# Four spacer tiles that shift tile addresses modulo 256 bytes in a one-core hybrid decoder layer

## The chip, the cores and the metric

The kernel runs on one core of a Trainium2 chip. The metric is the time of one execution on the device in microseconds (us), as the median of several runs. A profile of one execution shows which engine did what and when: PE is TensorE (matmul), PEld its loading of weights, DVE is VectorE, ACT ScalarE, POOL GpSimd, SP the engine that issues most transfers. Numbers such as L158 are lines of the kernel.

## The reference

The kernel computes one layer on a sequence of 1024 tokens of width 1024, in float32:

```python
hn = rmsnorm(x, attn_norm_w)
proj = hn @ w_in                                   # 1024 x 3592
da_q, da_k, da_v, ml_qk, ml_v, ml_o, ml_i, ml_f = split_projection(proj)
da_out = diff_attention(da_q, da_k, da_v, lam, slopes)   # 4 heads, causal, ALiBi
da_out = rmsnorm(da_out, diff_norm_w) * (1.0 - lam_init)
qk = silu(causal_dwconv(ml_qk, mlstm_conv_w, mlstm_conv_b))
h = mlstm_chunkwise(mq, mk * ML_DIM ** -0.5, mv, i_pre, logf)   # 4 heads
ml_out = sigmoid(ml_o) * rmsnorm(h, mlstm_norm_w)
x = x + concatenate([da_out, ml_out]) @ w_out
u = causal_dwconv(rmsnorm(x, ffn_norm_w) @ w_up, ffn_conv_w, ffn_conv_b)   # D_FF = 2816
gate, up = split(u, 2)
x = x + (silu(gate) * up) @ w_down
return rmsnorm(x, final_norm_w)
```

## The kernel before

**Products.** A float32 operand is split into a high and a low part in a rounded type (fp32r), and each product is three matmuls: high by high, high by low, low by high. `mm3` (L157) keeps the two halves of a weight tile in the array and streams the token tile; `mm3b` (L162) keeps the token tile in the array and streams the weight tile. A matmul has 128 rows, 128 columns of weights and, nearly always, 512 streamed columns. While one streams, PEld reads the weights of the next from the on-chip memory (SBUF).

**Stages.** In order of time:

- Projections: x transposed and normalised is split into 16 tiles `xb` (L208, pool `px`). Columns of w_in come through `wf`, are split into `w` (8 buffers, pool `wp`, L121), and are multiplied by `xb`. The gates are 32 matmuls with `wg16` as weights, 16 columns for each block kc of 128 inputs (L411). While these run, POOL forms sums of weight blocks that later stages use (L327).
- mLSTM in eight chunks, then attention in 32 steps of a head and 128 tokens. The query and key projections of a head, which still read `xb`, are put between the steps. In the last head `px` is closed, and `px2` and `pmx` open at its place.
- Output projection: `mixT` (L799) loads a row block of the mixed heads into `mx`, transposes it on PE against an identity in `cst` and splits it into `mxT`; `mxT` is then held in the array, and `w` or `th` (the weights of the attention half) stream.
- MLP, up: a seven-product scheme in place of eight block products. The tokens stand in blocks: B11 and B21 in `hb` (pool `ph0`), B22 in `B22h` and `B22l`, and the sums T1 to T4 with their high parts in `th` and their low parts in `raw` (all pool `phn`) or in `x2a` (pool `px2`). Sums of weights are made on POOL by `up_sums` (L968 to L970), in tiles `s` and `wu` of pool `pf`, which takes the place of `pmx`. `product` (L1013) issues the matmuls.
- MLP, down: a second scheme of the same kind from `wf`, `bw`, `a12`, `a21`, `a22`, split into `w`, and the final norm.

**Order.** The order of the work is written by hand in the program: each engine executes its instructions in program order, and waits on semaphores for those of others. SP issues the loads and stores in one queue.

**Addresses.** The pools are stacks. Those of the left side grow upwards from the pool below; those opened with `side="right"` grow downwards. Within a pool the first tile takes the lowest address. Sizes are rounded up to 32 bytes. One spacer exists already: `padr`, 64 bytes at the top of the right side. As built, nearly every large tile begins at 160 modulo 256; the exceptions are `cst` (128), `vext` (96 and 128 for its two buffers) and `Cst` (64). The slices that a matmul reads are whole multiples of 512 bytes in, so they keep the tile's place; only `wg16` steps by 64 bytes from one kc to the next, and the slices of `vext` and `Cst` by 516 bytes.

`Scope` (L51) is a pool that can be closed by hand:

Of the kernel before, what the change touches and what calls it, by code (L numbers as in the profile page):

```python
# [17 lines left out]
P = 128  # L18
# [21 lines left out]
def tile_hybrid(ctx: ExitStack, tc: tile.TileContext, I: dict, out: bass.AP):  # L40
# [105 lines left out]
    def getw(ahead):  # L146
        n = used[0]
        used[0] += 1
        while len(made) < min(n + 1 + ahead, len(specs)):
            made.append(wpiece(*specs[len(made)]))  # L150
        return made[n]
# [14 lines left out]


    px = Scope("px")
    pr0 = Scope("pr0", side="right")
    pq = Scope("pq", side="right")  # L170
    pa = Scope("pa", side="right")
# [507 lines left out]
    def qk_units(h):  # L679

        hd = Head()

        def alloc():
            for n in ("qs0", "qs1", "ks0", "ks1", "kl"):
                setattr(hd, n, pat.t([P, S], F32R, n, 2))

        def proj(which, hf):
            if hf == 0:
                if which == "q":
                    alloc()  # L690
                hd.w = getw(1)
            ps = mmps()
            for kc in range(KC):
                st_mm(ps, hd.w, kc, hf)
            t = slice(hf * 512, (hf + 1) * 512)
            f = pat.t([P, 512], tag="qf", bufs=2)
            V.scalar_tensor_tensor(f, ps, -0.125 / SLOPE[h] if which == "q" else 1.0, RB[:, t], op0=ALU.mult, op1=ALU.mult)
            a0, a1 = (hd.qs0, hd.qs1) if which == "q" else (hd.ks0, hd.ks1)
            lo = pat.t([P, 512], F32R, "qlo") if which == "q" else hd.kl[:, t]
            for a, p in ((a0, slice(0, 64)), (a1, slice(64, 128))):  # L700
                A.activation(a[p, t], f[p, :], AF.Copy)
                (V if h == 0 else GP).tensor_tensor(lo[p, :], f[p, :], a[p, t].bitcast(F32), op=ALU.subtract)
            s0, s1 = (lo[0:64, :], lo[64:128, :]) if which == "q" else (a0[0:64, t], a1[64:128, t])
            nc.sync.dma_start(a0[64:128, t].bitcast(F32), s0.bitcast(F32))
            nc.sync.dma_start(a1[0:64, t].bitcast(F32), s1.bitcast(F32))

        return hd, [lambda w_=w_, f=f: proj(w_, f) for w_ in "qk" for f in range(2)]
# [8 lines left out]
    def pad_q(n):  # L716
        if n < len(seq):
            h, qt = seq[n]
            for c, a in ((0, heads[h].qs0), (1, heads[h].qs1)):
                r = slice(c * 64, (c + 1) * 64)  # L720
                GP.tensor_copy(qz[c][n % 2][r, :], a[r, qt * P:(qt + 1) * P])
# [10 lines left out]
    def attn_scores(h, qt):  # L732
        hd = heads[h]
        L = (qt + 1) * P
        qs_ = slice(qt * P, (qt + 1) * P)
        if qt == 0:
            st[h] = {"Z": sm8(16, "Z"), "ss": sm8(8, "ass")}
        e = st[h]
        if qt % 4 == 0:
            e["O", qt // 4] = pat.t([P, 4, P], tag="O", bufs=2)  # L740
        mn, mb_ = sm8(2, "mn"), sm8(2, "mb")
        pt = []
        for c in range(2):
            sps = big([P, S])
            z = qz[c][qt % 2]
            qs, ks = (hd.qs0, hd.ks0) if c == 0 else (hd.qs1, hd.ks1)
            for c0 in range(0, L, 512):
                js = slice(c0, c0 + max(256, min(512, L - c0)))
                PE.matmul(sps[:, js], qs[:, qs_], ks[:, js], start=True, stop=False)
                PE.matmul(sps[:, js], z, hd.kl[:, js], start=False, stop=True)  # L750
            s = pat.t([P, S], tag="s", bufs=4)
            V.tensor_tensor_reduce(s[:, :L], sps[:, :L], B0[:, S - L:S], op0=ALU.add, op1=ALU.min, accum_out=mn[:, c:c + 1], scale=1.0, scalar=3.0e38)  # L752
            V.tensor_scalar(mb_[:, c:c + 1], mn[:, c:c + 1], SLOPE[h], None, op0=ALU.mult)  # L753
            A.activation(s[:, :L], s[:, :L], AF.Exp, bias=mb_[:, c:c + 1], scale=-SLOPE[h], accum_out=e["Z"][:, c * 8 + qt:c * 8 + qt + 1])  # L754
            pt.append(s)
        e["p", qt] = pt

    def attn_out(h, qt):
        e = st[h]
        L = (qt + 1) * P  # L760
        pt = e.pop(("p", qt))
        cc = sm8(1, "cc")
        V.reciprocal(cc, e["Z"][:, 8 + qt:9 + qt])
        V.scalar_tensor_tensor(cc, cc, nlam, e["Z"][:, qt:qt + 1], op0=ALU.mult, op1=ALU.mult)
        a = pt[0]
        V.scalar_tensor_tensor(a[:, :L], pt[1][:, :L], cc, a[:, :L], op0=ALU.mult, op1=ALU.add)
        ops = psA.t([P, P], tag="sb")
        for b0 in range(0, qt + 1, 4):
            nb = min(4, qt + 1 - b0)
            tps = psA.t([P, 512], tag="sa")  # L770
            for b in range(nb):
                PE.transpose(tps[:, b * P:(b + 1) * P], a[:, (b0 + b) * P:(b0 + b + 1) * P], ident)
            aT = pat.t([P, 512], tag="aT", bufs=2)
            A.activation(aT[:, :nb * P], tps[:, :nb * P], AF.Copy)  # L774
            for b in range(nb):
                k = b0 + b
                PE.matmul(ops, aT[:, b * P:(b + 1) * P], vda[k // 2][:, k % 2, h * P:(h + 1) * P], start=k == 0, stop=k == qt)  # L777
        o = e["O", qt // 4][:, qt % 4, :]
        A.activation(o, ops, AF.Square, accum_out=e["ss"][:, qt:qt + 1])
        A.activation(o, ops, AF.Copy)  # L780

    def attn_finish(h, q0, q1):
        n = q1 - q0
        e = st[h]
        r0, v = sm8(n, "r0"), sm8(n, "av")
        V.reciprocal(r0, e["Z"][:, q0:q1])
        V.tensor_tensor(v, r0, r0, op=ALU.mult)
        V.tensor_tensor(v, v, e["ss"][:, q0:q1], op=ALU.mult)
        y = rsqrt(meps(v, n, 128, "t"), n, "t")
        f = sm8(n, "af")  # L790
        V.tensor_tensor(f, y, r0, op=ALU.mult)
        o = e["O", q0 // 4][:, q0 % 4:q0 % 4 + n, :]
        GP.tensor_tensor(o, o, f.unsqueeze(2).broadcast_to([P, n, P]), op=ALU.mult)
        nc.sync.dma_start(mixed[q0:q1, :, h * P:(h + 1) * P].rearrange("t p d -> p t d"), o)
# [4 lines left out]
    def mixT(tt, half, bank):  # L799
        m = pmx.t([P, 512], tag="mx", bufs=2)  # L800
        nc.sync.dma_start(m, mixed[tt, :, half * 512:(half + 1) * 512])
        tps = bank()
        for i in range(4):
            PE.transpose(tps[:, i * P:(i + 1) * P], m[:, i * P:(i + 1) * P], ident)
        t = pmx.t([P, 2, 512], F32R, "mxT", 2)
        A.activation(t[:, 0, :], tps, AF.Copy)
        V.tensor_tensor(t[:, 1, :], tps, t[:, 0, :].bitcast(F32), op=ALU.subtract)
        return t
# [8 lines left out]
    def add_proj(tt, t, w):  # L817
        xx = x2[tt]
        for hf in range(2):
            ps = mmps()  # L820
            oproj(t, w, hf, ps)
            c = slice(hf * 512, (hf + 1) * 512)
            V.tensor_tensor(xx[:, c], xx[:, c], ps, op=ALU.add)

    def load_x2(tt):
        xx = px2.t([P, D], tag="x2a" if tt < 4 else "x2b", bufs=4)
        nc.sync.dma_start(xx, I["x"][tt])
        x2.append(xx)

    def oml_unit(tt):  # L830
        if tt == 0:
            w_oml.extend(getw(0) for i in range(4))
        load_x2(tt)
        add_proj(tt, mixT(tt, 1, mmps), w_oml)
# [4 lines left out]
    for n, (h, qt) in enumerate(seq):  # L839
        if qt == 0:  # L840
            if h < H - 1:
                heads[h + 1], fill = qk_units(h + 1)
            else:
                px.close()
                px2 = Scope("px2")
                pmx = Scope("pmx")
                fill = [lambda tt=tt: oml_unit(tt) for tt in range(NT - HELD)]
        if n + 1 < len(seq) and qt < NT - 1:
            attn_scores(*seq[n + 1])
        if fill and qt % 2 == 0:  # L850
            fill.pop(0)()
        pad_q(n + 2)
        if n + 1 < len(seq) and qt == NT - 1:
            attn_scores(*seq[n + 1])
        attn_out(h, qt)
        if h == H - 1 and qt % 2:
            attn_finish(h, qt - 1, qt + 1)
        elif h < H - 1 and qt % 4 == 3:
            attn_finish(h, qt - 3, qt + 1)

    pat.close()
    pr0.close()
    ph0 = Scope("ph0", side="right")
    phn = Scope("phn", side="right")


    fnw = pmx.t([P, D], tag="fnw")
# [490 lines left out]
```

## Time and profile before

| what | value |
|---|---|
| median of two runs | 1214.47 us (1214.32 to 1214.63) |
| profiled execution, its own time | 1213.26 us |
| its span, first to last instruction | 1211.5 us |
| mean granted clock of PE | 0.995 |
| HBM traffic | 116.02 MB read, 37.78 MB written |

The page gives shares of the span by engine, a row of 40 slices, transfers, the chain of work that ended last, and the costliest groups of instructions. In a group, the first number behind the bar is the time in which at least one instruction of the group ran, and the second the mean length of one. Matmuls overlap, so the length of one is more than the spacing from one start to the next. The places of the busiest groups by tile:

```profile
L116 DVE TENSOR_TENSOR w<-wf,w 128x512 fp32r<-128x512 f32 x128 | 108.4, 858 | 27.9 <-ACT w L115 21.7
L158 PE MATMUL mm<-xb,w 128*128 128x512 f32 x168 | 66.1, 394 | 0.0
L163 PE MATMUL big<-w 128*128 128x512 f32 x132 | 51.5, 390 | 0.8 <-DVE x L1202 0.8
```

The first row is the vector half of the weight split, the second a projection product (xb streamed, w held), the third a product of the down stage with w on both sides.

### The profile page before, as it was taken

The numbers are of one execution on the slowest core, as the hardware profiler recorded it, in microseconds if no ns is written. First come the engines' busy times: TensorE is split into PE (matmuls) and PEld (weight loads), VectorE is DVE, ScalarE is ACT, GpSimd is POOL, SyncE is SP. The second block draws the span as 40 slices with busy tenths as digits, with TensorE's granted clock in tenths as the row PEclk, the third lists the DMA queues.
The fourth block names the chain that finished last, engine by engine and source line by source line (L and its number), as shares of the span: only waits on it lengthen the run. The fifth ranks groups of instructions, "written<-read, shape, count | busy, mean of one in ns | idle before, by whom it ended". The sixth has DMA issues, their size and how long they took to land.

```text
span 1211.5 us, 15939 instructions
## 1 busy us (share of the span) xinstructions
PE 1183.0 (98%) x5622; PEld 973.3 (80%) x5622; DVE 899.2 (74%) x1564; ACT 571.0 (47%) x1114; POOL 480.1 (40%) x364
## 2 busy tenths in 40 slices
PE   9998999999999999999999999999999999999996
PEld 7885788888778878888888888888888888888885
DVE  5598232566767777669998998788887878886694
ACT  6534323334666666344644444434344345544462
POOL 0475451003543431001198887888887600000000
PEclk9998999999999999999999999999999999999999
DMA  8755664124212243332322312222222169823223
GB/s 307 252 206 205 226 243 166 62 71 157 79 52 54 70 157 114 121 127 99 124 70 87 103 72 100 91 70 87 77 80 104 54 217 346 296 96 96 96 79 139
DMA packets 61743, 159.03 MB, mean 131 GB/s; under 512 B 6176, under 2 KB 10464, under 8 KB 61664
## 3 DMA queue, kind: packets, MB, share of 16 engines
q1 hardware_dynamic: 61232, 157.21, 38.0%
q8 instruction: 44, 0.72, 0.3%
q10 hardware_dynamic: 432, 0.82, 0.2%
q14 instruction: 35, 0.29, 0.1%
HBM read 116.02 MB, written 37.78 MB: 127 GB/s over the span
## 4 chain that ended last, share of the span: by engine, by line
PE 84%; DVE 5%; DMA 3%; ACT 3%; POOL 3%; issue 1%; SPq 1%; POOLq 0%; ACTq 0%; DVEq 0%
PE mm L160 6%; PE mm L158 6%; PE mm L159 6%; PE mm L163 5%; PE mm L164 5%; PE mm L165 5%; PE big L158 4%; PE big L160 4%; PE big L159 4%; PE big L164 4%; PE big L165 4%; PE big L163 4%; PE sb L777 3%; POOL vda L327 3%; PE sb L158 2%; PE sb L160 2%
## 5 line engine op out<-in xcount | busy, mean ns | idle before, releaser
L115 ACT ACTIVATE w<-wf 128x512 fp32r<-128x512 f32 x160 | 97.7, 624 | 142.3 <-POOL wf L999 33.6
L116 DVE TENSOR_TENSOR w<-wf,w 128x512 fp32r<-128x512 f32 x128 | 108.4, 858 | 27.9 <-ACT w L115 21.7
L1041 DVE SCALAR_TENSOR_TENSOR y<-x2b,fcw,y 128x1022 f32<-128x1022 f32 x44 | 91.8, 2125 | 0.0
L1040 DVE SCALAR_TENSOR_TENSOR y<-x2b,fcw,y 128x1023 f32<-128x1023 f32 x44 | 75.7, 1762 | 9.4 <-ACT y L1039 9.4
L116 POOL TENSOR_TENSOR w<-s,w 128x512 fp32r<-128x512 f32 x40 | 69.8, 1746 | 6.2 <-ACT w L115 6.2
L327 POOL TENSOR_TENSOR vda<-vda 128x512 f32<-128x512 f32 x24 | 46.6, 1958 | 63.7 <-DMA vda<-in_w_down_dram 62.9
L116 POOL TENSOR_TENSOR w<-wf,w 128x512 fp32r<-128x512 f32 x32 | 46.9, 1469 | 57.0 <-ACT w L115 47.2
L116 POOL TENSOR_TENSOR w<-wu,w 128x512 fp32r<-128x512 f32 x40 | 66.5, 1662 | 1.8 <-ACT w L115 1.8
L158 PE MATMUL mm<-xb,w 128*128 128x512 f32 x168 | 66.1, 394 | 0.0
L160 PE MATMUL mm<-xb,w 128*128 128x512 f32 x168 | 65.9, 392 | 0.0
L159 PE MATMUL mm<-xb,w 128*128 128x512 f32 x168 | 65.9, 392 | 0.0
L968 POOL TENSOR_TENSOR s<-wu 128x512 f32<-128x512 f32 x20 | 36.5, 1825 | 58.0 <-DMA wu<-in_w_up_dram 58.0
L752 DVE CUSTOM_DVE_ANT_0 s<-big,B 128x128 f32<-128x128 f32 (+7 forms) x64 | 47.6, 755 | 13.7 <-PE big L750 12.3
L1039 ACT ACTIVATE y<-x2b,fcw 128x1024 f32<-128x1024 f32 x44 | 52.3, 1237 | 9.6 <-DVE x2b L1030 8.4
L754 ACT ACTIVATE s<-s,mb 128x128 f32<-128x128 f32 (+7 forms) x64 | 49.3, 772 | 11.2 <-DVE mb L753 10.0
L163 PE MATMUL big<-w 128*128 128x512 f32 x132 | 51.5, 390 | 0.8 <-DVE x L1202 0.8
L164 PE MATMUL big<-w 128*128 128x512 f32 x132 | 51.4, 389 | 0.0
L165 PE MATMUL big<-w 128*128 128x512 f32 x132 | 51.3, 389 | 0.0
L115 ACT ACTIVATE w<-wu 128x512 fp32r<-128x512 f32 x48 | 29.7, 625 | 40.1 <-PE mm L160 10.7
L777 PEld LDWEIGHTS sb<-vda,aT 128*128 128x128 f32 x288 | 36.2, 190 | 15.4 <-ACT aT L774 14.6
L777 PE MATMUL sb<-vda,aT 128*128 128x128 f32 x288 | 44.2, 289 | 3.7 <-ACT aT L774 3.1
L115 ACT ACTIVATE w<-hb 128x512 fp32r<-128x512 f32 x41 | 25.8, 630 | 44.9 <-PE big L165 19.8
(514 smaller groups left out, 3769.8 us busy)
## 6 DMA issues: line engine op xcount, KB each, us to landing
wf<-in_w_up_dram SPq DMA_DIRECT2D x22, 512.0 KB, 4.5
actd<-y SPq DMA_DIRECT2D x21, 512.0 KB, 2.6
wu<-in_w_up_dram SPq DMA_DIRECT2D x20, 512.0 KB, 3.4
wf<-in_w_st_dram SPq DMA_DIRECT2D x12, 512.0 KB, 4.2
vda<-in_w_down_dram SPq DMA_DIRECT2D x12, 512.0 KB, 6.6
wsum<-vda SPq DMA_DIRECT2D x12, 512.0 KB, 3.0
wf<-in_w_mv_dram SPq DMA_DIRECT2D x12, 512.0 KB, 5.3
wf<-wsum SPq DMA_DIRECT2D x12, 512.0 KB, 3.4
```

Of the source, the lines that this page charges most:

```text
L115: A.activation(dst[:, 0, :], src, AF.Copy)
L116: loeng.tensor_tensor(dst[:, 1, :], src, dst[:, 0, :].bitcast(F32), op=ALU.subtract)
L158: PE.matmul(ps, sh, mh, start=first, stop=False)
L159: PE.matmul(ps, sh, ml, start=False, stop=False)
L160: PE.matmul(ps, sl, mh, start=False, stop=last)
L163: PE.matmul(ps, sh, w[:, 0, :], start=first, stop=False)
L164: PE.matmul(ps, sl, w[:, 0, :], start=False, stop=False)
L165: PE.matmul(ps, sh, w[:, 1, :], start=False, stop=last)
L327: GP.tensor_tensor(dst, x_, y, op=ALU.subtract)
L777: PE.matmul(ops, aT[:, b * P:(b + 1) * P], vda[k // 2][:, k % 2, h * P:(h + 1) * P], start=k == 0, stop=k == qt)
L1040: V.scalar_tensor_tensor(y[:, 1:], u[:, :S - 1], cw[:, 1:2], y[:, 1:], op0=ALU.mult, op1=ALU.add)
L1041: V.scalar_tensor_tensor(y[:, 2:], u[:, :S - 2], cw[:, 0:1], y[:, 2:], op0=ALU.mult, op1=ALU.add)
```

## The change

Four tiles are allocated that no instruction writes or reads. A line number in the program after the change is one larger from the first spacer on, two larger from the second, and four larger behind the last.

```diff
     px = Scope("px")
+    px.t([P, 8], tag="pad")
     pr0 = Scope("pr0", side="right")
...
                 pmx = Scope("pmx")
+                pmx.t([P, 24], tag="pad")
                 fill = [lambda tt=tt: oml_unit(tt) for tt in range(NT - HELD)]
...
     ph0 = Scope("ph0", side="right")
+    ph0.t([P, 4], tag="pad")
     phn = Scope("phn", side="right")
+    phn.t([P, 24], tag="pad")
```

What each does to the places, by the allocations of the two built programs:

| pool | spacer | tiles | begin modulo 256, before | after |
|---|---|---|---|---|
| px | 32 bytes | xb | 160 | 192 |
| pmx | 96 bytes | mx, mxT, fnw | 160 | 0 |
| ph0 | 16 bytes, takes 32 | hb | 160 | 160 |
| phn | 96 bytes | raw, th, B22h, B22l | 160 | 128 |
| all others | none | w, wf, x2a, x2b, vda, mqk, s, wu, ... | | as before |

The right side grows downwards, and a pool's first tile is its lowest. So the spacer of `ph0` lies below `hb` and leaves it where it was, but pushes the pool opened next, `phn`, down by 32 bytes. The spacer of `phn` lies below the tiles of `phn`, and no pool is opened below it.

All engines have the same instructions in the same order. Two lists of waits differ, because a tile now overlaps other earlier tiles. The first is on POOL at the start of the MLP, where the first `up_sums` follows the last sums of the tokens; s is its sum tile, and a name such as DMAHW4 is the semaphore of one of eight groups of transfers. Before:

```order
L793 TENSOR_TENSOR O<-O,af 128x256 [waits DVE_49,Activation_49]
L934 TENSOR_TENSOR raw<-raw,x2a 128x2x128 [waits DVE_49,PE_49,Activation_49]
L934 TENSOR_TENSOR raw<-raw,x2a 128x2x128 [waits DVE_49,Activation_49] x7
L968 TENSOR_TENSOR s<-wu 128x512 [waits DMAHW3_49,DMAHW4_49,DMAHW2_49,DMAHW7_49,DMAHW1_49,PE_49]
L969 TENSOR_TENSOR s<-s,wf 128x512 [waits DMAHW4_49,DMAHW5_49,DMAHW0_49,DMAHW6_49,DVE_49,Pool_49]
L970 TENSOR_TENSOR wu<-wf,wu 128x512 [waits DMAHW1_49,DMAHW5_49,DVE_49,PE_49]
L999 TENSOR_TENSOR wf<-wf,s 128x512 [waits DMAHW2_49,DVE_49,Pool_49]
```

And after, on POOL at the same place:

```order
L794 TENSOR_TENSOR O<-O,af 128x256 [waits DVE_49,Activation_49]
L938 TENSOR_TENSOR raw<-raw,x2a 128x2x128 [waits DVE_49,PE_49,Activation_49]
L938 TENSOR_TENSOR raw<-raw,x2a 128x2x128 [waits DVE_49,Activation_49] x7
L972 TENSOR_TENSOR s<-wu 128x512 [waits DMAHW4_49,DMAHW3_49,DMAHW5_49,DMAHW2_49,DMAHW6_49,DMAHW1_49,DMAHW7_49,DMAHW0_49,PE_49]
L973 TENSOR_TENSOR s<-s,wf 128x512 [waits DMAHW4_49,DVE_49,Pool_49]
L974 TENSOR_TENSOR wu<-wf,wu 128x512 [waits DMAHW1_49,DMAHW5_49,DVE_49,PE_49]
L1003 TENSOR_TENSOR wf<-wf,s 128x512 [waits DMAHW2_49,DVE_49,Pool_49]
```

Three waits on transfers moved from the second instruction of `up_sums` to the first. The second difference is on SP in the last head of attention, where x2a (the residual rows) and mx are loaded. Before:

```order
L827 DMA x2a<-in_x_dram 128x1024 [waits DMAHW1_49,PE_49]
L801 DMA mx<-mixed 128x512 [waits DMAHW2_49]
L827 DMA x2a<-in_x_dram 128x1024 [waits DMAHW3_49,PE_49]
L801 DMA mx<-mixed 128x512 [waits DMAHW6_49,DMAHW4_49,PE_49]
L827 DMA x2a<-in_x_dram 128x1024 [waits DMAHW5_49]
```

And after, on SP at the same place:

```order
L828 DMA x2a<-in_x_dram 128x1024 [waits DMAHW1_49,PE_49]
L802 DMA mx<-mixed 128x512 [waits DMAHW2_49]
L828 DMA x2a<-in_x_dram 128x1024 [waits DMAHW3_49]
L802 DMA mx<-mixed 128x512 [waits DMAHW6_49,DMAHW4_49,PE_49]
L828 DMA x2a<-in_x_dram 128x1024 [waits DMAHW5_49]
```

The third load of x2a no longer waits for PE.

## The prediction

> **What bounds the kernel now.** I read the top of the page first, then the waits of PE, then windows over single stages.
>
> ```profile
> span 1211.5 us, 15939 instructions
> PE 1183.0 (98%) x5622; PEld 973.3 (80%) x5622; DVE 899.2 (74%) x1564; ACT 571.0 (47%) x1114; POOL 480.1 (40%) x364
> PEclk9998999999999999999999999999999999999999
> PE sa L411 <- ACT mqk L393: 5.9, 1, 5.9
> PE sb L777 <- ACT aT L774: 3.1, 5, 1.4
> PE sb L477 <- DVE gs L412: 2.0, 1, 2.0
> ```
>
> PE is busy for 98% of the span at full clock in nearly every slice, and its longest wait in the program is one of 5.9 us. A change that only moves addresses can therefore gain or lose in earnest only if it alters how fast PE takes one product after another. The next view shows that rate in stages with very different neighbours: two stretches of the MLP, the whole MLP with most of the last product, and the last product alone under full DMA load.
>
> ```profile
> core 0: us, PE busy (x) PEld busy (x) DVE busy (x) ACT busy (x) POOL busy (x), PEclk, DMA share, GB/s
> 640.00:1160.00 520.00, 520.00 (x2296) 430.58 (x2295) 430.36 (x487) 233.15 (x357) 267.69 (x161) 1.00 0.35 122
> 700.00:740.00 40.00, 40.00 (x178) 33.12 (x177) 36.68 (x35) 16.66 (x23) 34.03 (x22) 1.00 0.26 92
> 1000.00:1040.00 40.00, 40.00 (x178) 33.12 (x177) 32.22 (x53) 20.65 (x37) 0.00 (x0) 1.00 0.97 362
> ```
>
> A window also counts the two products that it cuts, so 520 us hold 2294 starts: one every 226.7 ns. With POOL busy for 34 of 40 us and DMA at 0.26, or with POOL idle and DMA at 0.97, the count in 40 us is the same 178. Neither the other engines nor the transfers disturb the spacing. What is left for an address to act on is PE alone: the weights of the next product are read while the current one streams its moving tile.
>
> **The change, term by term.** It adds no instruction and moves none. It gives new starts modulo 256 to xb (160 to 192), to mx, mxT and fnw (160 to 0), and to th, raw and B22 (160 to 128). The tiles they are multiplied with, w above all, stay at 160. Products that then read two tiles of unlike starts, by tile:
>
> ```profile
> 0.00:1211.50 1211.50, 328.24 (x1376) 0.99 0.38 131
> 0.00:1211.50 1211.50, 93.17 (x384) 0.99 0.38 131
> 0.00:1211.50 1211.50, 266.40 (x896) 0.99 0.38 131
> 0.00:1211.50 1211.50, 68.46 (x176) 0.99 0.38 131
> 0.00:1211.50 1211.50, 57.77 (x176) 0.99 0.38 131
> 0.00:1211.50 1211.50, 34.23 (x88) 0.99 0.38 131
> ```
>
> These are PE's instructions on xb, mxT, th, raw, B22h and B22l, over the whole span. Of th's 896, 192 have mxT as weights and are already in the 384. So 1376 + 384 + 704 + 176 + 176 + 88 = 2904 products are touched, about half of PE's 5622 matmuls. One nanosecond on each is 2.9 us, or 0.24%.
>
> *The price of one.* No 512-wide product with full weights has unlike starts in this trace: every one reads 160 against 160. Bounds come from other rows. Below: what the stream itself needs. At the gate products PE ran at half clock for a while:
>
> ```profile
> 105.90:106.72 0.82, 0.82 (x2) 0.50 0.00 0
> 105.90:109.28 3.38, 3.38 (x8) 0.50 0.00 0
> ```
>
> Six more starts in 2.56 us are 427 ns each at half clock, so 213.3 ns at full clock. The settled 226.7 has 13.3 ns on top of that, and an address effect could at most remove those. Above: the gate products, the only 512-wide ones whose weights change their start. wg16 steps by 64 bytes for each kc, so its starts run through 160, 224, 32 and 96 against xb at 160. Below stand the half of them that ran at full clock, an xb product with w for comparison, and both halves in the timeline:
>
> ```profile
> L411 PE MATMUL sb<-xb,wg x16: 390/396/398, 96.1 to 99.6; 128*16 128x512 f32 x16
> L159 PE MATMUL sa<-xb,w x24: 389/389/395, 40.7 to 90.2; 128*128 128x512 f32 x24
> 96.09 3.88 PE L411 MATMUL sb<-xb,wg 128*16 128x512 f32 x16
> 105.90 5.71 PE L411 MATMUL sa<-xb,wg 128*16 128x512 f32 x16 [5.92 <-ACT mqk L393]
> ```
>
> Fifteen spacings in 3.88 - 0.40 us are 232 ns each. A product's length here is its spacing plus 162 ns (389 against 226.7), so 390 to 398 are spacings of 228 to 236. None of the four distances makes a product shorter than the 389 of equal starts, and none is far longer; the four mix within one band of 8 ns. That band has another possible cause, because products with equal starts show it too for some two microseconds after PE changes its work:
>
> ```profile
> 340.21 0.47 PE L750 MATMUL big<-kl,qz 128*128 128x512 f32 x1
> 340.53 0.39 PE L158 MATMUL mm<-xb,w 128*128 128x512 f32 x1
> ...
> 342.38 0.39 PE L160 MATMUL mm<-xb,w 128*128 128x512 f32 x1
> ```
>
> From 340.53 to 342.38 eight spacings take 1.85 us, 231 ns each. So the trace ties 228 to 236 to a pattern that has not settled, with like starts as well as unlike ones. Narrow products say the same: mqk against mqk (160 on 160), vext (96 or 128 and up) on DT, Cst (64 and up) on qw:
>
> ```profile
> L611 PE MATMUL sb<-mqk 128*128 128x128 f32 x64 | 8.7, 276 | 0.0
> L619 PE MATMUL big<-vext,DT 128*128 128x129 f32 x64 | 12.1, 277 | 0.0
> L621 PE MATMUL big<-Cst,qw 128*128 128x129 f32 x56 | 10.8, 275 | 0.0
> ```
>
> They take 275 to 277 ns whatever the starts. They stream only a quarter as long, so they count for less. I take 0 ns per product, by the gate rows (no distance is quicker than the equal one) and these; the ends, -13.3 and +9.0 ns (398 against 389), go to the rivals.
>
> The row for the settled spacing is 226.7 ns. The Trainium skill (TensorE: Matmul & The Clock Gate, section "Wait — 56ns, not 53.3ns?") measures 426.7 ns cold and 215.7 ns warm for back-to-back 512-wide products. The cold figure agrees with the 427 above, the warm one does not; no run here shows 215.7, and by it 11.0 ns of each touched product could be taken away, 31.9 us in all, which would give 1182.6 us.
>
> *DVE, ACT and POOL on the moved tiles.* Where DVE already adds tiles of unlike starts (cst at 128, DT at 160) it takes as long as with like ones:
>
> ```profile
> L587 DVE TENSOR_TENSOR DT<-DT,cst 128x512 f32<-128x512 f32 x8 | 5.4, 691 | 11.4 <-DMA DT<-mwd 11.4
> L1202 DVE TENSOR_TENSOR x<-x,acc 128x512 f32<-128x512 f32 x12 | 7.8, 688 | 0.0
> ```
>
> 691 against 688: 3 ns, so for some 100 instructions on moved tiles 0.3 us even if PE waited for every one. I take 0.
>
> *The two changed waits.* POOL's first sum in the MLP (L968) now waits on all eight transfer semaphores, since its tile s begins to overlap both mx buffers; three of these stood at L969, the next instruction on POOL. POOL's further sums and the weight splits queue behind it, and PE needs the splits. SP's third x2a load drops a wait on PE that two earlier loads on SP have made.
>
> ```profile
> 601.85 1.55 POOL L968 TENSOR_TENSOR s<-wu 128x512 f32<-128x512 f32 x1 [20.78 <-DMA wu<-in_w_up_dram]
> L801 SPq DMA_DIRECT2D mx<-mixed x16: 319/326/439, 428.6 to 544.5; - x16
> DMA to landing us min/median/max: 2.7/3.5/4.8
> 441.93 0.44 SPq L801 DMA_DIRECT2D mx<-mixed  x1
> 442.46 0.38 SPq L827 DMA_DIRECT2D x2a<-in_x_dram  x1
> ```
>
> The last mx load is issued at 544.5 and lands by 549.3, 52 us before L968 starts, which is released by wu's load. SP's x2a load follows the mx load before it within 0.09 us of its end, so the dropped wait held nothing. Both 0. The mx loads keep their size and count; PE's list of waits names none of them, so 0.
>
> *Sum.* 1213.26 us (the profiled execution: 1211.5 span and 1.8 around it) + 0 = 1213.3. The runs' median is 1214.47, 1.2 us above that execution, so the forecast is 1214.5 us.
>
> **Rivals.** *A, faster.* The 13.3 ns above the stream are a clash of weights and moving tile that begin at the same place modulo 256; spread out, the 2904 products run at 213.3: 2904 x 13.3 = 38.7 us, 1175.8 us. For it: all 512-wide products with full weights have equal starts, and nothing in the trace names another cause of the 13.3. Against it: the gate rows at four distances. It decides for faster from 8.4 ns per product, a spacing of 218.3. The page's 1182.6 is a case of it. *B, slower.* Unlike starts hold the touched products in the unsettled pattern. At the 231 of the timeline row that is 2904 x 4.4 = 12.8 us, 1227.3 us; at the gate rows' 398 it is 2904 x 9.0 = 26.1 us, 1240.6 us. For it: wg16's starts change, and its products never settle within their sixteen. Against it: its median of 396 is short of the bar, since slower needs 8.4 ns, a spacing of 235.1 for all of them. *C, the change does less than it says.* phn's own spacer lies below its tiles and moves none of them, hb stays at 160, and so do the lows that are kept in x2a (none of these is among the 2904). Where starts do not matter this is the forecast itself, 1214.5 us.
>
> **How the numbers follow.** Two per cent are 24.3 us, about what a measurement of this kernel can tell from no change. No effect (C included): 0.72, at 1212 to 1217, since a half-clock stretch like that of the second gate half (5.71 us against 3.88) may come or go for about 2 us. A in full: 0.07. A in part, up to a quarter of the 13.3 ns (9.7 us, 1205): 0.06. B at 231: 0.09. B above 235: 0.06. Faster is 0.07, slower 0.06, same 0.72 + 0.06 + 0.09 = 0.87. The range takes in A in part and B at 231, 1204 to 1228, and leaves out A in full and B above 235.
>
> **What would show it.** Right: 178 products in 700 to 740 us as before, xb and th rows at 389 ns, the gate rows at 390 to 398, the same 5.9 us wait. A: rows of xb, th and raw at 376 to 381 while x2a and hb stay at 389, and more than 180 products in that window. B: those rows at 393 or more. The forecast is wrong if the touched rows leave 389 while the untouched stay.

## The result, and the profile after the change

The changed kernel takes 1230.74 us (two runs, 1230.65 to 1230.82) against 1214.47. The ratio is 1.0135, with a 95% interval of 1.0115 to 1.0156: 16.3 us slower. The interval leaves out 1, so the change is clear of noise, though it is less than the two per cent that the prediction took for the limit of what can be told. The time lies above the range of 1204 to 1228 that was forecast.

The top of the page after the change:

```profile
span 1228.8 us, 15937 instructions
...
PE 1201.8 (98%) x5622; PEld 974.9 (79%) x5622; DVE 896.8 (73%) x1564; ACT 572.1 (47%) x1114; POOL 473.0 (38%) x364
...
PEclk9999999999999999999999999999999999999999
```

PE is busy for 18.8 us longer (1201.8 against 1183.0) with the same 5622 matmuls at the same mean clock (0.995 in both), and the span is 17.3 us longer. So PE's idle time shrank, by 1.5 us, and the loss lies wholly inside the matmuls. (The two instructions fewer are separate waits, one on POOL and one on SP.) The waits of PE show where the 1.5 us went:

```profile
PE sa L412 <- ACT mqk L394: 4.3, 1, 4.3
```

The longest wait, 5.9 us before, is 4.3. PE comes 2.7 us later to the first half of the gate products (98.8 us against 96.1), but the second half, which waits for ACT, starts only 1.1 us later (107.0 against 105.9). In the four runs below in which xb keeps the place of w, this wait is 5.3 to 5.9 us. The windows, with the same columns as in the prediction:

```profile
640.00:1160.00 520.00, 520.00 (x2261) 424.36 (x2261) 417.37 (x467) 229.70 (x344) 273.61 (x166) 1.00 0.34 121
700.00:740.00 40.00, 40.00 (x174) 32.48 (x173) 31.66 (x30) 17.48 (x24) 32.11 (x20) 1.00 0.30 102
```

174 products in 40 us where 178 stood, and 2261 in 520 us where 2296 stood. The next view is PE's busy time by tile over the whole span, in the order xb, mxT, th, raw, B22h, B22l and, as the seventh, x2a, whose place did not change:

```profile
0.00:1228.80 1228.80, 336.63 (x1376) 0.99 0.38 129
0.00:1228.80 1228.80, 95.13 (x384) 0.99 0.38 129
0.00:1228.80 1228.80, 272.13 (x896) 0.99 0.38 129
0.00:1228.80 1228.80, 69.63 (x176) 0.99 0.38 129
0.00:1228.80 1228.80, 58.93 (x176) 0.99 0.38 129
0.00:1228.80 1228.80, 34.80 (x88) 0.99 0.38 129
0.00:1228.80 1228.80, 69.22 (x176) 0.99 0.38 129
```

Against the rows of the prediction: xb +8.4, mxT +2.0, th +5.7, raw +1.2, B22h +1.2, B22l +0.6. Of these, some 0.7 us stand twice (th streamed while mxT is held). That leaves 18.3 us on the 2904 touched products. Not all of it is the price of an address, because xb's row holds two changes of the clock. The second half of the gates, part of it at half clock, took 5.20 us where it took 5.71. And behind the next wait, one of 2.4 us at 126 us, seven products on xb start 427 ns apart, as at half clock, where before none did. That stretch costs about 1.5 us and stands in three groups, of which one is shown (before, then after):

```profile
L163 PE MATMUL sa<-w,xb 128*128 128x512 f32 x32 | 12.7, 396 | 0.0
...
L163 PE MATMUL sa<-w,xb 128*128 128x512 f32 x32 | 13.5, 421 | 0.0
```

Without the two, some 17.3 us are left, about 6 ns for each touched product. x2a, whose 176 products stood at 68.46 us before, lost 0.8 us more. The groups of the same kernel (busy time, then the mean length of one) show the touched and the untouched side by side:

```profile
L158 PE MATMUL mm<-xb,w 128*128 128x512 f32 x168 | 66.9, 398 | 0.0
...
L163 PE MATMUL big<-w 128*128 128x512 f32 x132 | 51.5, 390 | 0.8 <-DVE x L1206 0.8
...
L158 PE MATMUL big<-th,w 128*128 128x512 f32 x120 | 47.5, 396 | 0.0
...
L159 PE MATMUL big<-hb,w 128*128 128x512 f32 x64 | 24.9, 389 | 0.0
...
L159 PE MATMUL mm<-x2a,w 128*128 128x512 f32 x60 | 23.6, 393 | 0.0
```

The group of xb went from 394 to 398 ns. th on w, at 389 before, is now at 396; hb on w, issued by the same line in the same stage, is at 389; w on w (the down stage) is at 390, as before. The spacing from one start to the next, taken from the trace, is 234 ns for th and 233.3 for raw and B22 where it was 226.7. x2a is slowed without having been moved: its products stand between two of th, and their spacing rose from 226.6 to 231.1.

### The profile page after: what moved, and what is told of

It is laid out like the page before. It is cut to its first block, busy times and chain, and to the rows that moved or that the text cites. A ratio compares the mean times of both kernels' runs of the same rounds, so it can differ in the third digit from the quotient of the medians.

```text
span 1228.8 us, 15937 instructions
## 1 busy us (share of the span) xinstructions
PE 1201.8 (98%) x5622; PEld 974.9 (79%) x5622; DVE 896.8 (73%) x1564; ACT 572.1 (47%) x1114; POOL 473.0 (38%) x364
## 4 chain that ended last, share of the span: by engine, by line
PE 84%; DVE 5%; DMA 3%; ACT 3%; POOL 3%; issue 1%; SPq 1%; POOLq 0%; ACTq 0%; DVEq 0%
PE mm L160 6%; PE mm L158 6%; PE mm L159 6%; PE mm L163 5%; PE mm L164 5%; PE mm L165 5%; PE big L159 4%; PE big L160 4%; PE big L158 4%; PE big L163 4%; PE big L164 4%; PE big L165 4%; PE sb L778 3%; POOL vda L328 3%; PE sb L158 2%; PE sa L158 2%
## 5 line engine op out<-in xcount | busy, mean ns | idle before, releaser
L116 DVE TENSOR_TENSOR w<-wf,w 128x512 fp32r<-128x512 f32 x128 | 105.9, 838 | 28.0 <-ACT w L115 22.5
L1045 DVE SCALAR_TENSOR_TENSOR y<-x2b,fcw,y 128x1022 f32<-128x1022 f32 x44 | 88.6, 2052 | 0.0
L972 POOL TENSOR_TENSOR s<-wu 128x512 f32<-128x512 f32 x20 | 33.1, 1654 | 60.8 <-DMA wu<-in_w_up_dram 40.0
L115 ACT ACTIVATE w<-s 128x512 fp32r<-128x512 f32 x43 | 27.0, 629 | 47.3 <-PE big L160 15.9
L1034 DVE TENSOR_TENSOR x2b<-x2b,mm 128x512 f32<-128x512 f32 x51 | 34.1, 681 | 19.5 <-PE mm L160 18.7
```

What stands on the lines that cost most here:

```text
L115: A.activation(dst[:, 0, :], src, AF.Copy)
L116: loeng.tensor_tensor(dst[:, 1, :], src, dst[:, 0, :].bitcast(F32), op=ALU.subtract)
L1045: V.scalar_tensor_tensor(y[:, 2:], u[:, :S - 2], cw[:, 0:1], y[:, 2:], op0=ALU.mult, op1=ALU.add)
```

## The experiments

Three theories went into them. **T**: a 512-wide product in the rounded four-byte type (fp32r) is slower by some 6 ns when the weights and the streamed tile do not begin at the same place modulo 256 bytes; only this relation counts. **P**: it is the place that counts, and 160 happens to be a good one. **W**: the two changed lists of waits, or a shifted order in time, cost the loss. The time before was measured again beside each run on the same chip.

### The parts alone

First the spacer of `px` alone. It moves xb from 160 to 192 and is the one that brings SP's changed wait.

```diff
     px = Scope("px")
+    px.t([P, 8], tag="pad")
```

> Only the 32-byte spacer of px: xb begins at 192, all else at 160. Theory T (a product is slow when the weights being read and the streamed tile begin at unlike places modulo 256): the 1344 xb products with full weights go from 389 to about 397 ns, all other products stay at 389; the sum over the rows of xb in the trace after the change was 8 us, so 1222 to 1223 us. Theory W (the loss comes from the two changed waits, which do not lie in this stage): 1214.5 us. Theory S (the loss comes from the sums' tiles alone): 1214.5 us.

Measured: 1219.51 us (10 runs) against 1215.39 (19 runs), ratio 1.0029, 95% 1.0018 to 1.0040, so about 3.5 us, less than half of what xb's rows lost in the whole change. Two groups, the top of the page and the wait at the gates:

```profile
L158 PE MATMUL mm<-xb,w 128*128 128x512 f32 x168 | 67.0, 399 | 0.0
...
L158 PE MATMUL big<-th,w 128*128 128x512 f32 x120 | 46.7, 389 | 0.0
```

```profile
PE 1190.4 (98%) x5622; PEld 973.7 (80%) x5622; DVE 901.1 (74%) x1564; ACT 571.5 (47%) x1114; POOL 478.3 (39%) x364
```

```profile
PE sa L412 <- ACT mqk L394: 3.8, 1, 3.8
```

xb is at 399 and th back at 389. PE is busy for 7.4 us more, as T says, but this execution's span (1215.1 us) is only 3.6 us longer. The other 3.8 us came out of PE's idle time. It arrives later at the gates and waits 3.8 us there where it waited 5.9, which is 2.1 us; and the wait of 2.0 us for gs behind the gates is gone in this execution. The direction was foreseen, the size was not, because the expectation counted the products and left out that slack. The expectation also places both changed waits elsewhere, although SP's comes with this spacer. It costs nothing: from the last product on xb to the first on mxT, the stretch in which x2a and mx are loaded, 8.85 us pass before, in this run and in the whole change.

Then the spacer of `ph0` alone, as 32 bytes. It pushes all of `phn` (raw, th, B22) from 160 to 128 and changes no list of waits.

```diff
     ph0 = Scope("ph0", side="right")
+    ph0.t([P, 8], tag="pad")
```

> Only the spacer of ph0: th, raw and B22 begin at 128, all else at 160. T: rows of th, raw and B22 at 394 to 397 ns, xb rows back at 389, the MLP's 700 to 740 us hold 174 products in place of 178, sum about 9 us over before: 1223 us. W: 1214.5, since neither list of waits changes here as it did there. If only the front stage pays: 1214.5.

Measured: 1224.56 us (4 runs) against 1215.39, ratio 1.0070, 1.0054 to 1.0087. Its windows and groups:

```profile
640.00:1160.00 520.00, 520.00 (x2262) 424.36 (x2261) 420.55 (x469) 230.04 (x348) 267.65 (x162) 1.00 0.34 120
700.00:740.00 40.00, 40.00 (x174) 32.42 (x174) 32.50 (x30) 16.89 (x23) 32.91 (x20) 1.00 0.23 79
```

```profile
L158 PE MATMUL big<-th,w 128*128 128x512 f32 x120 | 47.5, 396 | 0.0
...
L159 PE MATMUL big<-raw,w 128*128 128x512 f32 x64 | 25.3, 396 | 0.0
...
L159 PE MATMUL big<-hb,w 128*128 128x512 f32 x64 | 24.9, 389 | 0.0
```

The MLP has the rate of the whole change without either changed wait. From the first product on hb to the last one of the up stage PE takes 430.2 us, 429.8 in the whole change and 421.1 before. There is no slack in this stage, so the loss stays.

Last the spacer of `pmx` alone (mxT from 160 to 0), which brings POOL's changed waits.

```diff
                 pmx = Scope("pmx")
+                pmx.t([P, 24], tag="pad")
```

> Only the spacer of the mixed tokens' pool is kept; the 384 products that stream mxT begin 96 bytes further modulo 256, and the list of waits of one POOL instruction at the start of the MLP changes as in the whole change. T (unlike starts cost about 6 ns a product, whatever else moves): mxT's 384 products take 2 to 2.5 us more in the rows (95.1 to 95.7 us of PE's busy time against 93.2), everything else streams at 227, 178 products in 700 to 740 us; part of it may be taken up at the gates, so 1215.5 to 1217 us, against about 1215 before. W (the changed wait costs): a loss at the start of the MLP beyond what the rows of mxT show, with mxT's own rows as they were.

Measured: 1217.33 us (11 runs) against 1215.18 (15 runs), ratio 1.0015, 1.0005 to 1.0024. (In these products mxT is held, and w or th streams; the expectation has it the other way round.) PE's busy time on mxT, and the window in the MLP:

```profile
0.00:1215.50 1215.50, 95.34 (x384) 1.00 0.38 131
```

```profile
700.00:740.00 40.00, 40.00 (x178) 33.14 (x177) 36.27 (x32) 17.37 (x24) 33.20 (x21) 1.00 0.25 86
```

mxT costs 2.2 us more, and the time is longer by about as much: 2.2 us between the medians, 0.6 to 2.9 by the interval. The MLP runs at 178 again, and from the first product on hb to the last one of the up stage PE takes 421.0 us (421.1 before), so nothing is left for the changed wait. The profiled execution itself is 4.0 us longer than the one before; the half-clock stretch behind the gates, which it too has, is part of that. The three ratios add up to 1.0114. The combined half-width of the three is 0.0022 and that of the whole is 0.0020, so they agree with its 1.0135, though no more closely than that: the 192 products of th on mxT are slow in two of the parts.

### The relation or the place

If the place counts, moving everything to 192 must hurt as well. Here the spacer at the bottom of the left side moves all of that side up by 32 bytes, and the halved `padr` moves the right side up by as much.

```diff
-    ctx.enter_context(tc.tile_pool(name="pad", bufs=1, side="right")).tile([P, 16], F32, name="padr")
+    ctx.enter_context(tc.tile_pool(name="pad", bufs=1, side="right")).tile([P, 8], F32, name="padr")
...
     wp = Scope("wp")
+    wp.t([P, 8], tag="pad")
```

> Every tile that PE reads in a 512-wide product is moved by the same 32 bytes: a spacer below w on the left, the spacer at the top of the right side cut from 64 to 32 bytes. All begin at 192; cst alone stays at 128. T (only the relation counts): 389 ns everywhere, 1214.5 us. Theory P (160 is a good place in itself, 192 and 128 are bad ones): all some 4600 products at 395 to 397 ns, 25 to 30 us more, about 1240 us.

Measured: 1215.70 us (10 runs) against 1215.39, ratio 1.0001, 0.9992 to 1.0011.

```profile
700.00:740.00 40.00, 40.00 (x178) 33.12 (x177) 38.88 (x33) 17.76 (x26) 35.06 (x21) 1.00 0.23 79
```

Every group is back at the lengths of before, but for the few products beside the waits at the gates. Then the left side alone: w, xb, mxT and x2a at 192, and th, raw, B22 and hb left where they were.

```diff
     wp = Scope("wp")
+    wp.t([P, 8], tag="pad")
```

> The spacer lies below w on the left side alone: w, xb, mxT, x2a and the tiles of the down stage go to 192 together, th, raw, B22 and hb on the right stay at 160. T: xb products stay at 389 though xb has moved; th, raw, B22 and now hb too go to 394 to 397 though they have not moved; x2a, streamed between th, about 393; down stage 389. Some 10 us from th, raw, B22 and x2a with the MLP and the attention half of the output projection, and 3 us from the 528 hb products: 1226 to 1229 us. Theory P (a tile is slow when it has left 160): xb and the down stage slow, hb and th at 389.

Measured: 1227.91 us (4 runs) against 1214.95 (13 runs), ratio 1.0109, 1.0082 to 1.0136. Three groups:

```profile
L159 PE MATMUL mm<-xb,w 128*128 128x512 f32 x168 | 66.2, 394 | 0.0
...
L159 PE MATMUL big<-th,w 128*128 128x512 f32 x120 | 47.5, 396 | 0.0
...
L159 PE MATMUL big<-hb,w 128*128 128x512 f32 x64 | 25.3, 396 | 0.0
```

xb moved and is as fast as before (394 in both), since w moved with it. th and hb did not move and are slow, at 396. hb, which the change had left alone, now pays too. P falls, and W with it, since neither of the two changed waits is in this run.

The last of this kind puts xb at 224, 64 bytes beyond w:

```diff
     px = Scope("px")
+    px.t([P, 16], tag="pad")
```

> xb at 224, 64 bytes past w, the rest as before. By the measured row of distances (64 bytes past: 229.2 ns a product, 192 bytes past, which is 64 before: 233.3): products that stream xb at about 391 to 392, products that hold xb and stream w at about 395 to 396. If the distance counts only as like or unlike: both at 396. About 3 to 5 us over before, since the wait at the gates takes up part.

Measured: 1218.93 us (8 runs) against 1214.95, ratio 1.0033, 1.0018 to 1.0047.

```profile
L158 PE MATMUL mm<-xb,w 128*128 128x512 f32 x168 | 66.5, 396 | 0.0
...
L163 PE MATMUL mm<-w,xb 128*128 128x512 f32 x96 | 38.8, 404 | 0.0
```

Where xb streams, 64 beyond its weights, a product is milder than at 32 (396 here, 399 there; median spacings of 226 to 231 by line). Where xb is held and w streams, the distance is -64, and the group is as slow as at 32 (404, against 400 before). Its median spacing is 233 to 234. The sign of the distance counts, as in the row of distances below.

### The price by itself

To measure the price alone, 400 products were put ahead of the kernel: one tile of weights and eight tiles to stream, each beginning 32 bytes further than the last, forty products on each. They add work and change none; the time of the program says nothing here.

```diff
+    wt = bt.t([P, 4, P], F32R, "wt")
+    rs = [bt.t([P, 520], F32R, f"r{n}") for n in range(8)]
...
+    for r in (rs[0], *rs, rs[0]):
+        pb_ = psB.t([P, 512], tag="bench", bufs=2)
+        for k in range(40):
+            PE.matmul(pb_, wt[:, k % 4, :], r[:, 0:512], start=k == 0, stop=k == 39)
```

> 400 products of 512 columns are put ahead of the kernel: weights wt at 160 (four slices in turn, 512 bytes apart), and eight streamed tiles r0 to r7 that begin 32 bytes apart, 40 products each, r0 (160, like the weights) once more at the end. T modulo 256: r0 at 389 ns once it runs at full clock, r1 (192) and r7 (128) at 394 to 397, the others unlike too, none under 389. Had the period been 128 or 64 bytes, r4 or r2, r4 and r6 would be at 389. Rival A of the prediction, some distance at which the 13.3 ns go: a group at 376 to 385. The whole takes about 90 us longer; its time is not compared.

Each window below runs from the first start of one group to the first start of the next, so it holds forty spacings (distances 0, 32, 64, then 160 and 224):

```profile
15.10:24.16 9.06, 9.06 (x41) 7.51 (x40) 1.00 0.99 360
24.16:33.50 9.34, 9.34 (x42) 7.50 (x40) 1.00 0.93 310
33.50:42.66 9.16, 9.16 (x41) 7.51 (x40) 1.00 0.73 296
...
61.33:70.70 9.37, 9.37 (x42) 7.53 (x41) 1.00 0.89 328
...
80.03:89.36 9.33, 9.33 (x42) 7.51 (x40) 1.00 0.13 50
```

Divided by forty, with windows read to 0.01 us and so to some 0.3 ns: 226.5 ns at the same place (226.7 from the single starts), 233.5 at 32, 229.0 at 64, 234.3 at 160, 233.3 at 224; 96, 128 and 192 lie at 233.2 to 233.5. None of the eight is quicker than the same place, which ends rival A of the prediction. That 64 would be so much milder than the others had not been expected. The DMA share ranges from 0.13 to 0.99, and the two distances of 32 bytes either way cost the same at 0.93 and at 0.13. Back on the first tile after the eighth, the spacings are 230, 236, 229, 232, 231 and then 226.7: like starts need some five products to settle.

A second set asked for smaller distances, for 256 bytes, for starts that alternate, and for fewer columns of weights. The groups differ in one expression, the slices:

```diff
+        PE.matmul(b, wk(k), rt[:, 1:513], start=k == 0, stop=k == 39)
...
+        PE.matmul(b, wk(k), rt[:, 64:576], start=k == 0, stop=k == 39)
...
+        PE.matmul(b, wk(k, k % 2 * 8), rt[:, k % 2 * 8:k % 2 * 8 + 512], start=k == 0, stop=k == 39)
...
+        PE.matmul(b, wk(k, k % 2 * 8), rt[:, (k + 1) % 2 * 8:(k + 1) % 2 * 8 + 512], start=k == 0, stop=k == 39)
```

> Groups of 40 products ahead of the kernel, weights at 160 in slices 512 bytes apart unless said. Streamed tile at the same place: 389 ns. 4, 8, 16 bytes past it: if what counts is a line of 16 bytes, the first two stay at 389 and the third goes to 394 or more. 240 bytes past: 394 or more. 256 past: 389 if the period is 256. Then two tiles each for weights and stream, 32 bytes apart and taken in turn. First, each product like in itself, so that the weights read during a stream (those of the next product) are unlike it: T (the stream against the weights that are being read) says 394 or more; a clash of a product with its own weights would leave 389. Second, each product unlike in itself, the next weights like the stream: T says 389, its rival 394 or more. The same weights slice each time: 389. Fewer columns of weights, 64 and 16, like: if the 13 ns above the bare stream are the reading of weights lines, they fall with the columns (to about 382 and 378); 16 columns 32 bytes off: 392 to 398 like the gate products. The whole takes some 120 us longer; its time is not compared.

In order of cost: 4 bytes off (L183), alternating with each product like its own weights and unlike the next (L198), 16 bytes off (L189), alternating the other way round (L201), 16 columns of weights at the same place (L210), 256 bytes off (L195), and the same slice of weights each time (L204):

```profile
L183 PE MATMUL bench<-rt,wt 128*128 128x512 f32 x40 | 9.6, 399 | 0.0
...
L198 PE MATMUL bench<-rt,wt 128*128 128x512 f32 x40 | 9.4, 395 | 0.0
L189 PE MATMUL bench<-rt,wt 128*128 128x512 f32 x40 | 9.4, 394 | 0.0
...
L201 PE MATMUL bench<-rt,wt 128*128 128x512 f32 x40 | 9.4, 393 | 0.0
...
L210 PE MATMUL bench<-rt,wt 128*16 128x512 f32 x40 | 9.3, 391 | 0.0
L195 PE MATMUL bench<-rt,wt 128*128 128x512 f32 x40 | 9.3, 390 | 0.0
L204 PE MATMUL bench<-rt,wt 128*128 128x512 f32 x40 | 9.2, 389 | 0.0
```

A distance of 256 is as good as none once it has settled (226.7), and one of 4 bytes is the worst (spacing 236.6); 8 and 240 bytes, whose groups are not shown, are at 233.2 and 233.3. So the period is 256, and 4 bytes are not too small a step to matter. Two expectations were missed. Whether a product must be like its own weights or like the next one's is not told apart: neither alternation comes to 389 (232.2 and 230.6 from start to start). And fewer columns of weights do not take the extra away in proportion. At the same place the spacing is 230.0 with 64 columns and 228.9 with 16, not less than 226.7; with 16 columns 32 bytes off it is 231.3, so there 32 bytes make 2.4 ns.

The third set asked how far the finding reaches: other widths of the stream, and a two-byte type (bf16).

```diff
+        PE.matmul(b, wk(0), rt[:, 8:520], start=k == 0, stop=k == 39)
...
+        PE.matmul(b, wk(k), rt[:, 0:256], start=k == 0, stop=k == 39)
...
+        PE.matmul(b, wk(k), rt[:, 8:264], start=k == 0, stop=k == 39)
...
+        PE.matmul(b, wh(k), rb[:, 0:512], start=k == 0, stop=k == 39)
...
+        PE.matmul(b, wh(k), rb[:, 16:528], start=k == 0, stop=k == 39)
```

> The kernel before with 520 products put ahead of it: groups of forty on tiles of ones whose places are known, so the time is longer by about 120 us and says nothing; the rows do. What is asked is how far the finding reaches. Rounded four-byte type, 512 columns, all weights from one slice, the stream 32 bytes off: 231 to 235 ns by T, since the weights are read again for each product; 227 if only a change of slice costs. 256 and 128 columns, at the same place and 32 bytes off: if the extra is paid once per product (T1), about 6 ns at each width; if it is paid per column streamed (T2), about 3 and 1.5 ns. Two-byte type, 512 columns, at the same place and 8, 32, 64 and 128 bytes off: T1 again about 6 ns where unlike; if it goes by the bytes that are read, about 3; 0 if it belongs to the rounded four-byte type alone.

The groups, in order: 512 columns 32 bytes off with weights from one slice (L187); bf16 at the same place (L205), 32 off (L208), 128 off (L214) and 64 off (L211); 256 columns at the same place (L190) and 32 off (L193):

```profile
L187 PE MATMUL bench<-rt,wt 128*128 128x512 f32 x40 | 9.5, 395 | 0.0
...
L205 PE MATMUL bench<-rb,wb 128*128 128x512 bf16 x40 | 8.8, 379 | 0.0
L208 PE MATMUL bench<-rb,wb 128*128 128x512 bf16 x40 | 8.8, 379 | 0.0
L214 PE MATMUL bench<-rb,wb 128*128 128x512 bf16 x40 | 8.8, 379 | 0.0
L211 PE MATMUL bench<-rb,wb 128*128 128x512 bf16 x40 | 8.8, 379 | 0.0
...
L190 PE MATMUL bench<-rt,wt 128*128 128x256 f32 x40 | 5.0, 283 | 0.0
L193 PE MATMUL bench<-rt,wt 128*128 128x256 f32 x40 | 4.9, 280 | 0.0
```

With weights from one slice the spacing is 233.4, so a change of slice is not what costs. In bf16 the spacing is 215.8 ns at each of the four places, so the effect belongs to the four-byte type. In that type the extra is neither per product nor per column: at 256 columns the same place is even a little slower than 32 bytes off (120.0 against 118.0), and at 128 columns both settle at the same 111.7. Both T1 and T2 fall.

What remains open is why the same place is good at 512 columns. The four-byte weights take longer to load (188 ns in the records, against 98 in bf16), which would fit two reads that get in each other's way and fall into a quick rhythm only from like starts. But narrower weights at the same place are slower, not faster, the 256-wide products turn it round, and the alternations were undecided, so this stays a guess.

## Why the prediction was wrong

**The price of one: this step failed.** The prediction set a touched product at 0 ns. It measured about 6 ns in the rows. The count of 2904 was right, but for 32 gate products among them whose starts were mixed already. The right row was quoted. Fifteen gate spacings of 232 ns, the only 512-wide ones with unlike starts, lie 5.3 ns above 226.7; times 2904 that is 15.4 us, 1229.9 us, against 1230.74. That this comes out so close is partly luck. The gate products have 16 columns of weights and four distances mixed, and 32 bytes made only 2.4 ns with 16 columns; it is the sign and the order of size that the row had right. The prediction put this row down to "a pattern that has not settled, with like starts as well as unlike ones", because eight products with like starts took 231 ns each. Such a transient exists, but like starts leave it: five products in the row of distances. The gate products did not leave it in sixteen, which the prediction noted and gave to the rival. That was the difference to read.

**The narrow products** were given as the second support, since they take 275 to 277 ns whatever their starts. They do, and with 128 columns placed by hand both starts settle at 111.7 ns as well. But this says nothing of 512 columns: at 256 the two starts differ, with the sign turned. The prediction itself said that narrow products stream only a quarter as long and so count for less, which was reason enough not to lean on them.

**Rival A (faster)** fell. None of the distances tried is below 226.7, so the 13.3 ns above the bare stream are no clash of like starts. The bf16 products, at 215.8, put 11 of the 13.3 ns down to the four-byte type. The Trainium skill (TensorE: Matmul & The Clock Gate, section "Wait — 56ns, not 53.3ns?") gives 215.7 ns for a warm 512-wide product; the 215.8 in bf16 agrees with it, the 226.7 of fp32r does not. The prediction had let its figure stand as something that a better address might reach; what it takes is another type.

**Rival B (slower)** was what happened, between its two prices: 231 (1227.3 us) and 236 (1240.6 us) stood there, and the touched groups came to median spacings of 232 to 235. It had 0.15, and the range reached only to its lower price.

**The rest of the sum held.** The changed waits cost nothing: the loss in the MLP is the same without them (the spacer of `ph0` alone), the spacer of `pmx`, which brings POOL's, leaves the MLP at its 421 us, and the 8.85 us around SP's stayed. The down stage, with w on both sides, kept its rate, and so did hb. The spacer of `phn` moved none of its own tiles. One thing was left out: the lows in x2a were counted as untouched, but standing between products with unlike starts they lost 4.5 ns each, 0.8 us. Two things beside the addresses nearly cancel. The half-clock stretch that "may come or go" came a second time, behind the gates, for about 1.5 us, and was 0.5 us shorter at the gates. And the waits around the gates, which the prediction did not price as slack, took back 1.5 us of PE's 18.8, and 3.8 of 7.4 when xb alone was moved (one execution each).

## What to carry to other kernels

Where PE runs back to back on 512-wide four-byte products, let every tile that is held (128 columns) and every tile that is streamed against it begin at the same place modulo 256 bytes, and look for groups of 393 to 399 ns beside groups of 389 to find those that do not. A pool opened or resized elsewhere on the stack can break this without touching a single instruction of the products. And where only one row of a profile has the property that a change will spread, take its duration as the price, and explain it away only with a row that stays in that state as long.

## What the runs showed of the hardware

- A 512-wide fp32r product with 128 columns of weights takes 226.7 ns from start to start with weights and stream at the same place modulo 256 bytes, 229 with the stream 64 bytes further, and 231.6 to 236.6 at the other distances tried, of 4 bytes and up.
- The relation counts, not the place: all at 192 is as fast as all at 160 (ratio 1.0001).
- In bf16 the same product takes 215.8 ns at each of four distances.
- At 256 columns the fp32r product is 2 ns quicker 32 bytes off than at the same place (118.0 against 120.0); at 128 columns both take 111.7.
- At the same place, 512 wide, fewer columns of weights are slower: 230.0 ns with 64 and 228.9 with 16, against 226.7 with 128.
- Products with like starts need about five to settle after unlike ones, and like ones among unlike ones are slowed as well (x2a, 231.1).
- Behind the gates PE ran seven or eight products at half clock (427 ns apart) after a wait of 2.4 to 2.8 us, in four runs, and none after one of 1.9 to 2.3 us, in three.
